# The low parts of split weights computed on VectorE instead of GpSimd in a hybrid decoder step

## The chip, the core and the metric

The kernel runs on one core of one Trainium2 chip. The metric is the time of the program on the device in microseconds; the median of 3 runs of the kernel before is 2004.66 us (1998.97 to 2009.29). The engines are named as in the profile: PE is TensorE (matrix products; PEld its weight loads), DVE is VectorE, ACT is ScalarE, POOL is GpSimd, SP is SyncE, which issues most transfers.

## What is computed

One step of a one-layer decoder for a prompt of 1024 rows and 8 sample rows, with a width of 1024 and float32 inputs. The reference, cut to its frame:

```python
q, k, v, logf, u, z = mixer_inputs(rmsnorm(xp, g_mix), w_in, b_f, g_sgu_v)
xp = xp + merge_heads(fox_prompt(q, k, v, logf), sgu_prompt(u, z, w_s, b_s), g_att_out, g_sgu_out, w_o)
mk, mv = memory_kv(mem_prompt, g_mem, w_ck, w_cv)
xp = xp + cross_attend(rmsnorm(xp, g_cross), mk, mv, w_cq, w_co)
f, conv_p = conv_ffn(rmsnorm(xp, g_ffn), zeros, w_up, conv_w, conv_b, w_down)
xp = xp + f
...
att = fox_sample(q, k, v, logf, cache_k, cache_v, cache_logf, page_table)
...
y_prompt = rmsnorm(xp, g_final); y_sample = rmsnorm(xs, g_final)
```

`fox_prompt` is causal attention with 8 heads of 64 and forget gates, `sgu_prompt` a gating that mixes rows within chunks of 128, `cross_attend` attention with 4 heads into 256 memory rows, and `conv_ffn` a gated MLP (hidden width 2816) with a causal convolution of width 3. The 8 sample rows take the same layer, each attending to 8192 past rows of a paged cache.

## The kernel before

**Split products.** The large products of the prompt run with operands that are split in two: a high part, which ACT writes as a rounded copy (L215), and a low part, the remainder of the source minus the high part (L216). A product is then the sum of three matrix products, high by high, high by low and low by high (`gemm3`, L250, L251, L252; in p1 also L402 to L404). `split` does the splitting. For activations that carry a scale, the remainder is one instruction at L219, always on DVE.

**Weights.** `wload` brings a block of weights of 128 x 1024 (some 128 x 512 or 128 x 1040) into a raw buffer `wr` by a transfer on SP's queue, and calls `split`, which writes `wh` and `wl`. There are 4 raw buffers, 5 for the high and 4 for the low part (`WR`, `WH`, `WL`). `wload` has a kind of weight as argument, and a small table `POOL` says which share of the remainders of a kind is computed on GpSimd: all of `up`, `down` and `o`, none of `p1`. `o` stands for the output projections and the query projection of the cross-attention. An accumulator, `pool_acc`, turns the share into single choices.

**Stages of the prompt.** p1 projects the 1024 rows (to 270 us of the profiled execution or so); then attention and gating for the first half of 512 rows, then attention for the second. From 530 us on, each half goes in turn through the merge of heads and the output projection `out_proj`, the cross-attention `cross`, and the feed-forward `ffn`. In `out_proj` four blocks of weights make up one half of the output columns; four row tiles use all four of them, and a residual addition on DVE (L888) and a sum of squares on ACT (L207) follow each. `rows_rstd` makes the norm's factor from it: an addition (L893), a scaled addition (L200) and a power on GpSimd (L201); `norm_T` scales the rows (L928), transposes on PE (L937, L944) and splits (L218, L219). In the merge the transposes are L834. In `ffn` a block of `w_up` gives one tile of 128 hidden columns: 24 matrix products, then ACT (L1068) and DVE (L1069, L1070) for the convolution, and the product with the gate (L1077), whose result is split (L215, L216). Groups of 6, 6, 5 and 5 pairs of tiles are followed by the products with `w_down` and residual additions (L1102).

**The sample path in the background.** The 128 steps over the cache are interleaved with the prompt at a pace per stage (`PACE`). In each `kstep`, GpSimd issues a gather of 1 MB of keys (L1183), DVE or, for odd steps below 50, GpSimd multiplies by the query (L1191), and DVE sums (L1195). In each `vstep`, GpSimd issues a gather of values (L1244) and PE multiplies by the weights (L1250). Four buffers `kv` serve both. At the end of each of the 8 sample rows a softmax goes back and forth between PE and DVE (L1208, L1214, L1217, L1218, L1220, L1227, L1232, L1238). The rest of the sample path (its projections, cross-attention and feed-forward) follows until the end.

**Order.** Every engine works through its own queue in a fixed order. The order is made ahead of time by a planner that simulates the program: an instruction enters its engine's queue when its inputs and its buffer would be ready, earlier program text first. `tc.issue_after` and `tc.high_priority` change that for some instructions of the sample path and of the residuals.

Of the kernel before, what the change touches and what calls it, by code (L numbers as in the profile page):

```python
# [7 lines left out]
F32 = mybir.dt.float32  # L8
# [10 lines left out]
P = 128  # L19
# [64 lines left out]
def build(nc, tc, ctx, a, phases=None):  # L84
# [121 lines left out]
        j = tpool.tile([P, 1024], BF16, tag="junk", bufs=1, name=nm("junk"))[: src.shape[0], :n]  # L206
        nc.scalar.activation(j, src, AF.Square, accum_out=dst)  # L207

    POOL = {"up": 1.0, "down": 1.0, "p1": 0.0, "o": 1.0}
    pool_acc = [0.0]  # L210

    def split(src, h, l, scale=None, eng=None):

        if scale is None:
            nc.scalar.activation(h, src, AF.Copy)  # L215
            (eng or nc.vector).tensor_tensor(l, src, h.bitcast(F32), op=ALU.subtract)  # L216
        else:
            nc.scalar.activation(h, src, AF.Copy, scale=scale)  # L218
            nc.vector.scalar_tensor_tensor(l, src, scale, h.bitcast(F32), op0=ALU.mult, op1=ALU.subtract)  # L219
# [1 line left out]
    def WRAW(n):  # L221
        return spool.tile([P, SWID], F32, tag="wr", bufs=WR, name=nm("wr"))[:, :n]

    def wload(src, n, kind="p1"):

        pool_acc[0] += POOL[kind]
        eng = nc.vector
        if pool_acc[0] >= 1.0:
            pool_acc[0] -= 1.0
            eng = nc.gpsimd  # L230
        raw = WRAW(n)
        l = spool.tile([P, SWID], F32R, tag="wl", bufs=WL, name=nm("wl"))[:, :n]
        h = spool.tile([P, SWID], F32R, tag="wh", bufs=WH, name=nm("wh"))[:, :n]
        if len(src.shape) == 3:
            h = h.rearrange("p (a b) -> p a b", b=src.shape[2])
            l = l.rearrange("p (a b) -> p a b", b=src.shape[2])
            raw = raw.rearrange("p (a b) -> p a b", b=src.shape[2])
        nc.sync.dma_start(raw, src)
        split(raw, h, l, eng=eng)
        return h, l, raw  # L240

    def wpair(w, kk, c0, n):

        return w[kk * 256 : (kk + 1) * 256, c0 : c0 + n].rearrange("(k p) n -> p k n", p=P)
# [651 lines left out]
    def out_proj(w, mh, ml, xt, fetch=None):  # L896

        sq = squares()
        korder = (4, 5, 6, 7, 0, 1, 2, 3)
        for n in range(2):  # L900
            ws = {}
            for kk in (2, 3, 0, 1):
                ws[kk] = wload(wpair(w, kk, n * 512, 512), 1024, "o")
            if fetch and n == 0:
                xt += fetch()
            for i in range(4):
                tb = slice(i * P, (i + 1) * P)
                ps = MM()
                gemm3(
                    ps[:, :512],  # L910
                    [(mh[k][:, tb], ml[k][:, tb], ws[k // 2][0][:, k % 2, :], ws[k // 2][1][:, k % 2, :]) for k in korder],
                )
                residual(xt, sq, i, n, ps)
                hold[0] = n == 1 and i >= HI
                yield 5.2
        return sq
# [37 lines left out]
    def cross(xt, sq):  # L954

        hs, ls = yield from norm_T(xt, None, G_CROSS)
        r = rows_rstd(sq, 0, 4)
        rq = sm([P, 4], "rq", 2)
        nc.vector.tensor_scalar(rq, r, 1.0 / 16, None, op0=ALU.mult)
        q2 = []  # L960
        for n in range(2):
            ws = [wload(wpair(a["w_cq"], kk, n * 512, 512), 1024, "o") for kk in range(4)]
            for dt_ in range(4):
                if dt_ % 2 == 0:
                    q2.append(U([P, 2, 512]))
                ps = MM()
                cb = slice(dt_ * P, (dt_ + 1) * P)
                gemm3(
                    ps[:, :512],
                    [(ws[k // 2][0][:, k % 2, cb], ws[k // 2][1][:, k % 2, cb], hs[k], ls[k]) for k in range(8)],  # L970
                )
                nc.scalar.activation(q2[-1][:, dt_ % 2, :], ps[:, :512], AF.Copy)
                yield 5.2
        oh, ol = [], []

        def weigh(h):
            mkn = T2().rearrange("p (a b) -> p a b", b=256)
            hc = slice(h * MD, (h + 1) * MD)
            nc.sync.dma_start(mkn, mk_d[:, hc].rearrange("(a p) b -> p a b", p=P))
            mv = T2().rearrange("p (a b) -> p a b", b=256)  # L980
            nc.sync.dma_start(mv, mv_d[:, hc].rearrange("(a p) b -> p a b", p=P))
            tr = TR()
            for dd in range(2):
                for mt in range(2):
                    nc.tensor.transpose(
                        tr[:, dd * 256 + mt * P : dd * 256 + (mt + 1) * P], mkn[:, mt, dd * P : (dd + 1) * P], ident
                    )
            mkT = T2().rearrange("p (a b) -> p a b", b=256)
            nc.scalar.activation(mkT, tr.rearrange("p (a b) -> p a b", b=256), AF.Copy)
            mx = sm([P, 4], "cmx", 2)  # L990
            pp = U([P, 4, 256])
            l4 = sm([P, 4], "cl", 2)
            r4 = sm([P, 4], "cr", 2)
            for g in range(2):
                sv = BK().rearrange("p (i m) -> p i m", m=256)
                for i2 in range(2):
                    i = g * 2 + i2
                    for dd in range(2):
                        mmul(sv[:, i2, :], q2[h][:, dd, i * P : (i + 1) * P], mkT[:, dd, :], start=(dd == 0), stop=(dd == 1))
                g2 = slice(g * 2, g * 2 + 2)  # L1000
                nc.vector.tensor_reduce(mx[:, g2], sv, axis=AX.X, op=ALU.max, negate=True)
                nc.vector.tensor_tensor(mx[:, g2], mx[:, g2], rq[:, g2], op=ALU.mult)
                for i2 in range(2):
                    i = g * 2 + i2
                    nc.scalar.activation(pp[:, i, :], sv[:, i2, :], AF.Exp, bias=mx[:, i : i + 1], scale=rq[:, i : i + 1], accum_out=l4[:, i : i + 1])
            nc.vector.reciprocal(r4, l4)
            for i in range(4):
                nc.vector.tensor_scalar(pp[:, i, :], pp[:, i, :], r4[:, i : i + 1], None, op0=ALU.mult)
            return pp, mv

        def gather(pp, mv):
            pT = U([P, 2, 512])
            for mt in range(2):
                tr = TR()
                for i in range(4):
                    nc.tensor.transpose(tr[:, i * P : (i + 1) * P], pp[:, i, mt * P : (mt + 1) * P], ident)
                nc.scalar.activation(pT[:, mt, :], tr, AF.Copy)
            oh2, ol2 = U([P, 2, 512], F32R), U([P, 2, 512], F32R)
            for dd in range(2):
                ps = BK()  # L1020
                for mt in range(2):
                    mmul(ps, mv[:, mt, dd * P : (dd + 1) * P], pT[:, mt, :], start=(mt == 0), stop=(mt == 1))  # L1022
                split(ps, oh2[:, dd, :], ol2[:, dd, :])
                oh.append(oh2[:, dd, :])
                ol.append(ol2[:, dd, :])

        ahead = weigh(0)
        yield 4
        for h in range(MH):
            cur = ahead  # L1030
            if h < MH - 1:
                ahead = weigh(h + 1)
                yield 4
            gather(*cur)
            yield 5
        return (yield from out_proj(a["w_co"], oh, ol, xt))


    hlast = [const.tile([P, 2 * NF, 2], F32, tag=f"hlast{h}", name=f"hlast{h}") for h in range(2)]

    def ffn(hf, xt, sq, late=None):
# [12 lines left out]
        for gi, gn in enumerate(GROUPS):  # L1054
            gh, gl = [], []
            for f in range(f0, f0 + gn):
                hc2 = []
                for part in range(2):
                    ft = f + part * NF
                    h, l, _ = wload(a["w_up"][ft], 1024, "up")  # L1060
                    hv = h.rearrange("p (k c) -> p k c", c=P)
                    lv = l.rearrange("p (k c) -> p k c", c=P)
                    cw = [gp[:, CW + i * 44 + ft : CW + i * 44 + ft + 1] for i in range(3)]
# [22 lines left out]
            for n in range(2):  # L1086
                ws = []
                for k2 in range(0, gn, 2):
                    m = min(2, gn - k2)
                    r0 = (f0 + k2) * P  # L1090
                    h, l, _ = wload(
                        a["w_down"][r0 : r0 + m * P, n * 512 : (n + 1) * 512].rearrange("(k p) n -> p k n", p=P), m * 512, "down"
                    )
                    for q in range(m):
                        ws.append((h[:, q, :], l[:, q, :]))
                for i in range(4):
                    tb = slice(i * P, (i + 1) * P)
                    ps = MM()
                    gemm3(ps[:, :512], [(gh[k][:, tb], gl[k][:, tb], ws[k][0], ws[k][1]) for k in range(gn)])
                    if f0 + gn < NF:  # L1100
                        xs_ = xt[i][:, n * 512 : (n + 1) * 512]
                        nc.vector.tensor_tensor(xs_, ps[:, :512], xs_, op=ALU.add)  # L1102
                    else:
                        residual(xt, sq, i, n, ps)
                    yield 3.9
# [640 lines left out]
```

## Time and profile before

| | |
|---|---|
| median of 3 runs | 2004.66 us (1998.97 to 2009.29) |
| profiled execution | 1999.7 us, of which the span 1997.9 us |
| mean granted clock of PE | 0.958 |
| busy PE, DVE, POOL, ACT | 92%, 67%, 49%, 37% of the span |
| remainders of weights on POOL (L216) | 184, 450.0 us |
| remainders of weights on DVE (L216) | 36, 51.2 us |
| HBM | 258 GB/s over the span |

The profile is one execution, taken by the hardware profiler. A row of a group has the line of the kernel, the engine, the operation, what it writes and reads (buffer numbers left out), and how often; then the busy time in us and the mean of one in ns, or three durations in ns (minimum, median, maximum). After a second bar stands the idle time of the engine ahead of these instructions and what ended it. A row of the timeline has the start and the duration in us. A row of waits has the total, the number and the longest in us. Busy shares in the row of 40 slices are in tenths, each slice some 50 us. The granted clock is the share of its full rate that PE was given. Spans on POOL are rough.

### The profile page before, as it was taken

What the parts mean: (1) busy time and instruction counts of PE and PEld (TensorE: products, weight loads), DVE (VectorE), ACT (ScalarE), POOL (GpSimd) and SP (SyncE); (2) the same over time, 40 slices, a digit from 0 to 9 for tenths busy, and PEclk for the clock granted to TensorE, in tenths of its full rate; (3) what the DMA queues carried; (4) which work ended last, traced back from release to release, by engine and by line L of the source; (5) the groups of instructions that cost most, each with busy time, mean ns of one, the idle gap of its engine ahead of it and who ended that gap; (6) DMA issues with size and microseconds to landing.
All of it is one profiled execution on the core that took longest, in us unless ns stands there. A gap on an engine that the chain in (4) does not pass through costs nothing.

```text
span 1997.9 us, 24107 instructions
## 1 busy us (share of the span) xinstructions
PE 1838.5 (92%) x9159; PEld 1300.7 (65%) x9159; DVE 1332.5 (67%) x1467; ACT 732.9 (37%) x1344; POOL 988.4 (49%) x560
## 2 busy tenths in 40 slices
PE   8899989778999697999999999789999999899997
PEld 5777766556667455676777667566566668567773
DVE  3877456677677988998879999885424439532232
ACT  5332246566632322332323323322424423232331
POOL 1664343433387547676767576557243344233321
PEclk9999989889999898899999999899999999899999
DMA  8766786754497888888878889878664458666755
GB/s 322 258 235 229 270 318 229 251 172 154 165 356 263 306 296 311 297 309 312 313 279 329 292 296 336 328 259 306 259 225 162 141 192 268 239 197 224 258 204 191
DMA packets 160467, 517.05 MB, mean 259 GB/s; under 512 B 20168, under 2 KB 41928, under 8 KB 127584
## 3 DMA queue, kind: packets, MB, share of 16 engines
q0 software_dynamic: 38528, 270.88, 36.3%
q1 hardware_dynamic: 114912, 232.06, 33.6%
q10 hardware_dynamic: 6912, 12.59, 1.7%
q8 instruction: 72, 1.18, 0.2%
q14 instruction: 43, 0.35, 0.1%
HBM read 493.63 MB, written 21.84 MB: 258 GB/s over the span
## 4 chain that ended last, share of the span: by engine, by line
PE 65%; DVE 18%; DMA 6%; issue 5%; ACT 3%; POOL 2%; SPq 0%; POOLq 0%; ACTq 0%; DVEq 0%
PE ba L250 11%; PE ba L252 11%; PE ba L251 11%; PE bb L250 5%; PE bb L251 5%; PE bb L252 5%; DVE kv L1191 4%; PE dv L1250 4%; DVE s L1195 4%; DMA kv<-cache_k,kidx 2%; POOL wl L216 1%; DVE kv L1414 1%; PE dv L1493 1%; DMA kv<-cache_v,kidx 1%; PE ba L1022 1%
## 5 line engine op out<-in xcount | busy, mean ns | idle before, releaser
L216 POOL TENSOR_TENSOR wl<-wr,wh 128x1024 fp32r<-128x1024 f32 (+1 forms) x184 | 450.0, 2456 | 358.5 <-PE ba L252 211.6
L215 ACT ACTIVATE wh<-wr 128x1024 fp32r<-128x1024 f32 (+2 forms) x220 | 228.1, 1042 | 398.9 <-PE ba L251 105.1
L1191 DVE TENSOR_TENSOR kv<-kv,d 128x2048 f32<-128x2048 f32 (+1 forms) x109 | 308.7, 2836 | 42.6 <-DMA kv<-cache_k,kidx 42.4
L1183 POOL DMA_INDIRECT kv<-cache_k,kidx x128 | 175.8, 1373 | 287.4 <-PE dv L1250 110.3
L1195 DVE TENSOR_REDUCE s<-kv 128x32 f32<-128x2048 f32 (+1 forms) x139 | 292.1, 2107 | 29.4 <-POOL kv L1191 28.2
L1244 POOL DMA_INDIRECT kv<-cache_v,kidx x128 | 184.5, 1441 | 206.7 <-PE dv L1250 96.5
L250 PE MATMUL ba<-wh,u 128*128 128x512 f32 (+1 forms) x674 | 261.9, 390 | 7.1 <-ACT u L215 6.0
L251 PE MATMUL ba<-wl,u 128*128 128x512 f32 (+1 forms) x674 | 258.5, 384 | 1.3 <-DVE wl L216 1.3
L252 PE MATMUL ba<-wh,u 128*128 128x512 f32 (+1 forms) x674 | 257.6, 383 | 0.0
L250 PE MATMUL ba<-u,wh 128*128 128x512 f32 x568 | 231.3, 408 | 0.6 <-DVE u L219 0.5
L252 PE MATMUL ba<-u,wl 128*128 128x512 f32 x568 | 227.2, 401 | 0.0
L251 PE MATMUL ba<-u,wh 128*128 128x512 f32 x568 | 227.2, 400 | 0.0
L250 PEld LDWEIGHTS ba<-wh,u 128*128 128x128 f32 x674 | 128.1, 190 | 52.3 <-issue 17.8
L252 PEld LDWEIGHTS ba<-wh,u 128*128 128x128 f32 x674 | 127.8, 190 | 33.1 <-issue 7.5
L251 PEld LDWEIGHTS ba<-wl,u 128*128 128x128 f32 x674 | 128.2, 190 | 31.7 <-issue 6.5
L1250 PE MATMUL dv<-kv,s 128*32 128x512 f32 x1024 | 137.6, 627 | 5.5 <-DMA kv<-cache_v,kidx 5.5
L250 PEld LDWEIGHTS ba<-u,wh 128*128 128x128 f32 x568 | 108.9, 192 | 49.2 <-issue 14.3
L1191 POOL TENSOR_TENSOR kv<-kv,d 128x2048 f32<-128x2048 f32 (+1 forms) x30 | 117.0, 3908 | 43.9 <-DMA kv<-cache_k,kidx 38.7
L252 PEld LDWEIGHTS ba<-u,wl 128*128 128x128 f32 x568 | 108.5, 191 | 32.8 <-issue 7.6
L251 PEld LDWEIGHTS ba<-u,wh 128*128 128x128 f32 x568 | 108.7, 191 | 31.0 <-issue 5.9
L250 PE MATMUL bb<-wh,u 128*128 128x512 f32 (+1 forms) x318 | 125.5, 395 | 3.1 <-ACT u L215 1.5
L251 PE MATMUL bb<-wl,u 128*128 128x512 f32 (+1 forms) x318 | 123.3, 388 | 2.1 <-DVE wl L216 2.1
(395 smaller groups left out, 3079.1 us busy)
## 6 DMA issues: line engine op xcount, KB each, us to landing
wr<-w_up SPq DMA_DIRECT2D x88, 512.0 KB
kv<-w_up SPq DMA_DIRECT2D x22, 1024.0 KB
wr<-w_down SPq DMA_DIRECT2D x40, 512.0 KB
kv<-w_down SPq DMA_DIRECT2D x11, 1024.0 KB
wr<-w_in SPq DMA_DIRECT2D x16, 512.0 KB
wr<-w_o SPq DMA_DIRECT2D x16, 512.0 KB
wr<-w_cq SPq DMA_DIRECT2D x16, 512.0 KB
wr<-w_co SPq DMA_DIRECT2D x16, 512.0 KB
```

Of the source, the lines that this page charges most:

```text
L215: nc.scalar.activation(h, src, AF.Copy)
L216: (eng or nc.vector).tensor_tensor(l, src, h.bitcast(F32), op=ALU.subtract)
L250: mmul(out, sh, mh, start=(i == 0), stop=False)
L251: mmul(out, sh, ml, start=False, stop=False)
L252: mmul(out, sl, mh, start=False, stop=(i == n - 1))
L1022: mmul(ps, mv[:, mt, dd * P : (dd + 1) * P], pT[:, mt, :], start=(mt == 0), stop=(mt == 1))
L1183: nc.gpsimd.indirect_dma_start(kv, None, a["cache_k"], off(kidx[:, b, ch : ch + 1]))
L1191: eng.tensor_tensor(kvv[:, i : i + m, :], kvv[:, i : i + m, :], qb.unsqueeze(1).broadcast_to((P, m, 512)), op=ALU.mult)
L1195: nc.vector.tensor_reduce(s[:, ch * 4 + i : ch * 4 + i + m, :].rearrange("p k h -> p (k h)"), kvv[:, i : i + m, :].rearrange("p k (h d) -> ...
L1244: nc.gpsimd.indirect_dma_start(kv, None, a["cache_v"], off(kidx[:, b, ch : ch + 1]))
L1250: mmul(dv[32 * j : 32 * j + 32, :], s[:, ch * 4 : ch * 4 + 4, :].rearrange("p k h -> p (k h)"), kvv[:, j, :], start=(ch == 0), stop=(ch == ...
L1414: nc.vector.tensor_tensor(kn, kn, qb[n].unsqueeze(1).broadcast_to((P, 2, 512)), op=ALU.mult)
```

## The change

All remainders of split weights are computed on DVE: the table `POOL`, the accumulator and the arguments that carry them are removed, and `split` has no choice of engine. The 184 remainders at L216 that POOL computed, in `out_proj`, `cross` and `ffn`, go to DVE's queue. GpSimd keeps its gathers, the products of odd early cache steps (L1191), the copies in the attention of half 1 (L686) and the powers (L201). The number of buffers, the transfers and the high parts on ACT stay as they are. The planner makes the order anew.

```diff
-    POOL = {"up": 1.0, "down": 1.0, "p1": 0.0, "o": 1.0}
-    pool_acc = [0.0]
-
-    def split(src, h, l, scale=None, eng=None):
+    def split(src, h, l, scale=None):
 
         if scale is None:
             nc.scalar.activation(h, src, AF.Copy)
-            (eng or nc.vector).tensor_tensor(l, src, h.bitcast(F32), op=ALU.subtract)
+            nc.vector.tensor_tensor(l, src, h.bitcast(F32), op=ALU.subtract)
...
-    def wload(src, n, kind="p1"):
-
-        pool_acc[0] += POOL[kind]
-        eng = nc.vector
-        if pool_acc[0] >= 1.0:
-            pool_acc[0] -= 1.0
-            eng = nc.gpsimd
+    def wload(src, n):
+
...
-        split(raw, h, l, eng=eng)
+        split(raw, h, l)
...
-                ws[kk] = wload(wpair(w, kk, n * 512, 512), 1024, "o")
+                ws[kk] = wload(wpair(w, kk, n * 512, 512), 1024)
...
-            ws = [wload(wpair(a["w_cq"], kk, n * 512, 512), 1024, "o") for kk in range(4)]
+            ws = [wload(wpair(a["w_cq"], kk, n * 512, 512), 1024) for kk in range(4)]
...
-                    h, l, _ = wload(a["w_up"][ft], 1024, "up")
+                    h, l, _ = wload(a["w_up"][ft], 1024)
...
-                        a["w_down"][r0 : r0 + m * P, n * 512 : (n + 1) * 512].rearrange("(k p) n -> p k n", p=P), m * 512, "down"
+                        a["w_down"][r0 : r0 + m * P, n * 512 : (n + 1) * 512].rearrange("(k p) n -> p k n", p=P), m * 512
```

## The prediction

> **What bounds the kernel now.** I read the totals first, then the busy time by stage, the waits of TensorE, and the timeline at its longest waits.
>
> ```profile
> span 1997.9 us, 24107 instructions
> PE 1838.5 (92%) x9159; PEld 1300.7 (65%) x9159; DVE 1332.5 (67%) x1467; ACT 732.9 (37%) x1344; POOL 988.4 (49%) x560
> DVE  3877456677677988998879999885424439532232
> PEclk9999989889999898899999999899999999899999
> ```
> ```profile
> 530.00:590.00 60.00, 59.89 (x327) 44.45 (x325) 41.43 (x44) 26.78 (x50) 44.60 (x22) 1.00 0.94 356
> 590.00:810.00 220.00, 180.95 (x841) 118.20 (x840) 185.27 (x163) 64.63 (x123) 140.81 (x77) 0.89 0.80 295
> 810.00:1250.00 440.00, 432.30 (x1987) 308.27 (x1987) 396.56 (x303) 142.79 (x222) 302.21 (x164) 0.99 0.83 307
> 1250.00:1330.00 80.00, 64.16 (x312) 44.82 (x311) 68.72 (x47) 28.48 (x47) 50.94 (x27) 0.91 0.83 304
> 1330.00:1510.00 180.00, 162.83 (x772) 108.46 (x773) 90.67 (x107) 54.32 (x103) 84.67 (x52) 0.95 0.69 251
> 1510.00:1998.00 488.00, 467.21 (x2348) 327.69 (x2347) 200.40 (x304) 156.95 (x254) 156.79 (x72) 0.98 0.61 210
> ```
> The second block is by stage, with the columns PE, PEld, DVE, ACT, POOL, granted clock, DMA share, GB/s. The stages are: first output projection of half 0; its cross-attention; its feed-forward (810 to 1250); the turn to half 1; its cross-attention; its feed-forward. TensorE bounds the whole, at 92%. Where it isn't full (590 to 810, 1250 to 1510), DVE is what it stands behind, and the clock falls too (0.89, 0.91, 0.95). In the feed-forward of half 0 both run nearly full: PE 432.3 and DVE 396.6 of 440 us.
>
> ```profile
> PE ba L937 <- DVE u L928: 12.9, 2, 6.7
> PE bb L937 <- DVE u L219: 9.2, 2, 4.8
> PE ba L834 <- DVE rn2r L200: 8.9, 1, 8.9
> PE ms L1214 <- DVE pm L1208: 7.7, 2, 6.1
> PE ms L1227 <- DVE dg L1220: 4.4, 3, 3.4
> ```
> These are TensorE's longest waits on DVE from 530 to 1510 us (total, count, longest). None is on the remainder itself. Why DVE was late stands in the timeline; first DVE, then GpSimd, around the 8.9 us wait and around the 6.7 us one:
>
> ```profile
> 1250.24 9.38 DVE L1191 TENSOR_TENSOR kv<-kv,d 128x2048 f32<-128x2048 f32 x1 [1.04 <-DMA kv<-cache_k,kidx]
> 1260.21 2.27 DVE L1195 TENSOR_REDUCE s<-kv 128x32 f32<-128x2048 f32 x1
> 1250.45 7.02 POOL L216 TENSOR_TENSOR wl<-wr,wh 128x1024 fp32r<-128x1024 f32 x3
> 1263.13 1.11 PE L834 MATMUL ba<-cp,u 128*128 128x128 f32 x4 [8.89 <-DVE rn2r L200]
> ...
> 1490.59 11.14 DVE L928 TENSOR_SCALAR u<-u,rn0r 128x1024 f32<-128x1024 f32 x3 [2.48 <-POOL rn0r L201]
> 1490.55 9.30 POOL L216 TENSOR_TENSOR wl<-wr,wh 128x1024 fp32r<-128x1024 f32 x4
> ...
> 593.08 5.26 DVE L893 TENSOR_TENSOR rq<-sqx 128x4 f32<-128x4 f32 x1 [0.85 <-ACT junk L207]
> 588.87 9.45 POOL L216 TENSOR_TENSOR wl<-wr,wh 128x1024 fp32r<-128x1024 f32 x4
> ```
> An addition of four numbers a row (L893) lasts 5.26 us and ends when four GpSimd subtractions end (598.3). A product of 2.28 us (L1191) lasts 9.38 beside three of them. Three scalings (L928), 0.74 each at the median (next block of rows), last 11.14 beside four. GpSimd's remainders hold DVE up, and in bursts, because at the end of a projection three or four buffers come free almost at once. The Trainium skill (SBUF — State Buffer, "Who interferes with whom") has a rule for this: a DVE instruction with two SBUF inputs, or in a two-port mode, and a GpSimd instruction that reads SBUF exclude each other, while a reduction never takes part. The trace agrees: the reduction at 1260.21 takes 2.27 us. By the rule DVE would wait out one GpSimd instruction; 9.38 us is longer than that and covers all three, so the measurement decides.
>
> **What moves, and its price.** Every remainder of a weight from L216 goes from GpSimd's queue to DVE's: 176 of 128x1024 and 8 of 128x512. The p1 stage has 36 on DVE already and doesn't change. No DMA is moved.
>
> ```profile
> L928 DVE TENSOR_SCALAR u<-u,rn0r x6: 734/738/9818, 795.1 to 1501.0; 128x1024 f32<-128x1024 f32 x6
> L216 POOL TENSOR_TENSOR wl<-wr,wh x184: 1284/2413/4481, 536.1 to 1949.3; 128x1024 fp32r<-128x1024 f32 x176, 128x512 fp32r<-128x512 f32 x8
> L216 DVE TENSOR_TENSOR wl<-wr,wh x36: 1208/1226/5641, 8.2 to 343.6; 128x1024 fp32r<-128x1024 f32 x32, 128x1040 fp32r<-128x1040 f32 x4
> L1191 DVE TENSOR_TENSOR kv<-kv,d 128x2048 f32<-128x2048 f32 x97 | 294.5, 3037 | 42.5 <-DMA kv<-cache_k,kidx 42.4
> L1077 DVE TENSOR_TENSOR t<-t,t x44: 659/692/3505, 836.9 to 1935.6; 128x512 f32<-128x512 f32 x44
> L1077 DVE TENSOR_TENSOR t<-t,t 128x512 f32<-128x512 f32 x44 | 45.9, 1042 | 0.8
> L216 DVE TENSOR_TENSOR u<-t,u x44: 669/692/3127, 841.9 to 1937.0; 128x512 fp32r<-128x512 f32 x44
> L216 DVE TENSOR_TENSOR u<-t,u 128x512 fp32r<-128x512 f32 x44 | 43.1, 981 | 14.1 <-ACT u L215 14.1
> ```
> The rows give minimum/median/maximum in ns, or total and mean. One remainder costs GpSimd 2.41 us and DVE 1.23. Added to DVE: 176 x 1.23 + 8 x 0.69 (the same subtraction at 512 wide) = 222 us. Given back to DVE: L1191 97 x (3.04 - 2.28) = 74, L1077 44 x (1.04 - 0.69) = 15, the activations' remainders 44 x (0.98 - 0.69) = 13, L928 9, together 111 us; a little of L1191's is due to GpSimd's own products of the early steps and stays. So DVE's busy time goes to about 1332 + 222 - 111 = 1443 us, 72%. The price is in the stages, not there.
>
> Gain one, the five rows of waits: 12.9 + 9.2 + 8.9 + 6.1 + 3.4 = 40.5 us in seven places (of L1214 and L1227 only the longest; in each DVE had just been held by L216). What is late next there: the same three or four remainders, now 3.7 to 4.9 us of DVE in the same queue. If all stand ahead of the norm's instructions, 7 x 3.7 = 26 us come back and 14.5 are saved; if all stand behind, 40.5. The order isn't shown, but buffers come free while the last product still runs, so more of them will stand ahead than behind; I take two thirds ahead, which saves 23 us. Idle TensorE also costs clock: in the three stages with clocks of 0.89, 0.91 and 0.95 the lost time is 0.11 x 181 + 0.09 x 64 + 0.05 x 163 = 34 us for 39 + 16 + 17 = 72 idle, 0.47 us a us. With it 23 becomes **34 us saved** (21 to 60).
>
> Cost one, the feed-forward of half 0, where DVE has little room:
>
> ```profile
> 810.00:1250.00 440.00, 24.52 (x22) 163.01 (x65) 0.99 0.83 307
> 810.00:1250.00 440.00, 136.63 (x47) 0.00 (x0) 0.99 0.83 307
> 800.00:900.00 100.00, 96.17 (x432) 65.86 (x433) 95.79 (x78) 36.94 (x59) 69.27 (x38) 0.94 0.84 302
> ```
> The first row is of L216 alone (DVE, POOL), the second of L1191 alone, the third of a slice with all engines. 65 remainders add 65 x 1.23 = 80. L1191 gives back 136.6 - 47 x 2.28 = 29.5, and the two 512-wide groups about half of their 28. DVE then needs 396.6 + 80 - 43.5 = 433 of 440 us, 98%. In the third row it was 95.8% busy with TensorE at 96.2%; held to that, 433 / 0.958 = 452, **12 us more** (0 if it fills up, 36 if today's 43.4 us of idle stay beside the 433).
>
> Gain two: GpSimd also issues the gathers of the cache, and waits with them behind its remainders.
>
> ```profile
> PE ba L250 11%; PE ba L252 11%; PE ba L251 11%; PE bb L250 5%; PE bb L251 5%; PE bb L252 5%; DVE kv L1191 4%; PE dv L1250 4%; DVE s L1195 4%; DMA kv<-cache_k,kidx 2%; POOL wl L216 1%; DVE kv L1414 1%; PE dv L1493 1%; DMA kv<-cache_v,kidx 1%; PE ba L1022 1%
> 1051.97 4.62 POOL wl L216 x2
> 1056.91 9.75 DMA kv<-cache_k,kidx
> 1066.68 2.29 DVE kv L1191
> ```
> The chain of waits has 1% of its length, 20 us, in GpSimd's remainders, as here ahead of a gather that DVE then waits for. That goes; between 0 (the buffers free late anyway) and 20 I take **12 us**, which cancels cost one.
>
> Cost two, the 119 remainders outside that stage: each now waits its turn in DVE's queue, behind a cache step of two times 2.28 us, or, after 1510, behind instructions of the sample path that wait on TensorE. Four buffers hide most of it. The nearest rows are those of p1, who waited for the 36 that are on DVE:
>
> ```profile
>   PE bb L251: 2.1, 1
>   PE ba L251: 1.3, 1
> ```
> 3.4 us for 36, 0.094 each: 119 x 0.094 = 11, with the clock's 0.47 **16 us** (0 if the buffers hide all; 32 if DVE, fuller than in p1, doubles it). The waits that GpSimd's remainders had for TensorE's buffers cost nothing there, and DVE inherits them only where the order is wrong; that is within these bounds.
>
> Sum: -34 + 12 - 12 + 16 = -18. Against the profiled execution (1999.7 us, span 1997.9, 1.8 around it) that is 1982; the three runs have a median of 2004.66, 5 us above the profiled one, so the same step from the median gives 1987. The costs are more easily underrated than the gains, since a full in-order engine loses more than one slice shows; I lean 3 us that way: **1990 us**.
>
> **Rivals.** *DVE becomes the bound* (slower). For it: 98% needed from 810 to 1250, with TensorE at 98% beside it, and instructions queued in a fixed order. Against it: the 95.8% slice. If DVE keeps its 43.4 us of idle there, the stage is 36 longer, the rest costs 16 to 32, and of the gains only the 21 come: +31 to +47, so 2036 to 2052. It decides from some 25 us of kept idle on if gain two doesn't come: then costs pass gains (25 - 7 + 16 - 34 = 0, 7 being what 440 - 433 leaves). The Trainium skill (Perfetto Trace Analysis, "Optimizing Scalar/DVE Operations") would favour this rival: with a saturated DVE, handing work even to GpSimd may make sense; it adds that the two share an SBUF read port, so that it might not help.
>
> *Gains and costs cancel*: 34 + 12 against 12 + 32, about 2003. For it: the terms are of one size, and two of them are chosen between ends.
>
> *All remainders fall into DVE's gaps*: -60 - 12 + 0 + 0, 1933; with half of cost two 1941. Against it: the stages with stalls have DVE at 84% and 86%.
>
> *Transfers become the bound*: 307 GB/s over 440 us against the 356 of the stage from 530; the same bytes would fit in 379 us, so no.
>
> **How the numbers follow.** About 0.5% (10 us) is what can be told from no change. The forecast's case, moderate gain between 1960 and 1994, 0.37; the large gain 0.07; cancelling 0.18; DVE as the bound 0.38. So faster 0.44, same 0.18, slower 0.38. Both signs hold much of the chance: the range reaches from 1955 to 2042; the likeliest case's own is 1960 to 1994.
>
> **What would show it.** Right: the longest L1191 after 700 us falls from 9.38 to under 3 us; L893 stays under 1 us and L928 at 0.74; DVE 1420 to 1460 us busy; the five rows of waits at 23 us or less; clock above 0.91 from 590 to 810; the feed-forward of half 0 within 15 us of 440. Wrong: TensorE waiting for wl from DVE by more than 20 us in total, DVE at 97% with TensorE under 95% in that feed-forward, or the norm still late behind a run of L216 on DVE.

## The result and the profile after

| | before | after |
|---|---|---|
| median, 4 runs each | 2001.82 us (1995.63 to 2009.29) | 1973.22 us (1971.44 to 1979.7) |
| ratio, 95% interval | | 0.9874 (0.9843 to 0.9904) |
| span of the profiled execution | 1997.9 us | 1969.6 us |
| mean granted clock | 0.958 | 0.965 |

The change makes the kernel 1.3% faster, 28.6 us between the medians. The prediction had 14.7 us (1990 from 2004.66). Of the 28.3 us between the two spans, 18.6 are idle time of TensorE (159.4 before, 140.8 after) and 9.7 are its busy time: the same 9159 matrix products, at a granted clock of 0.965 instead of 0.958. First the totals of the kernel after, with the busy time in 40 slices. Lines that follow L216 in the text move up by 3 to 8 in it: the remainders of weights are L213, the cache products L1183 (before L1191), the gathers of keys L1175, the residual additions L880, the splits with a scale L216, the norm's scalings L920 and its transposes L929.

```profile
span 1969.6 us, 23939 instructions
PE 1828.8 (93%) x9159; PEld 1295.1 (66%) x9159; DVE 1395.3 (71%) x1651; ACT 730.1 (37%) x1344; POOL 538.0 (27%) x376
DVE  4877466786767798898989999988335549653442
PEclk9999989989999989899999999999999999999998
```

DVE has the 184 remainders more and only 62.8 us more busy time; GpSimd is at 27%. The same groups as before, in the kernel after, by shape (busy us, mean ns, then idle time ahead):

```profile
L213 DVE TENSOR_TENSOR wl<-wr,wh 128x1024 fp32r<-128x1024 f32 x208 | 258.1, 1252 | 168.3 <-PE ba L244 70.1 <-PE bb L244 35.0 <-PE ba L243 17.2
L1183 DVE TENSOR_TENSOR kv<-kv,d 128x2048 f32<-128x2048 f32 x97 | 234.1, 2414 | 24.8 <-DMA kv<-cache_k,kidx 23.7 <-issue 0.9
L1069 DVE TENSOR_TENSOR t<-t,t 128x512 f32<-128x512 f32 x44 | 30.0, 683 | 0.5
L213 DVE TENSOR_TENSOR u<-t,u 128x512 fp32r<-128x512 f32 x44 | 30.0, 684 | 10.9 <-ACT u L212 10.9
L920 DVE TENSOR_SCALAR u<-u,rn0r 128x1024 f32<-128x1024 f32 x6 | 4.1, 748 | 0.8 <-POOL rn0r L201 0.8
```

The groups of the feed-forward and of the norm that had been held are at their own durations again; the cache products are at 2.41 us on average. And here is the view of those products from 700 us on, instruction by instruction (minimum, median, maximum in ns), where GpSimd has no large product left:

```profile
L1183 DVE TENSOR_TENSOR kv<-kv,d x74: 2254/2282/2295, 701.8 to 1371.7; 128x2048 f32<-128x2048 f32 x74
```

None of these is held any more; before, one of 9.38 us stood there. The 62.8 us are what is left of 217.3 added (the remainders of weights on DVE went from 51.2 to 268.5 us in the groups by line), so 154.5 us were given back.

**Where the time came from.** Cut at the same instructions in both timelines (first residual addition of a projection, first and last convolution step on DVE of a feed-forward), in us, one execution of each kernel:

| stretch | before | after | difference |
|---|---|---|---|
| start to the residuals of the first output projection | 558.1 | 556.6 | -1.5 |
| from there, with cross-attention, to the first feed-forward | 270.0 | 272.5 | +2.5 |
| feed-forward of half 0, to its last tile | 397.1 | 381.9 | -15.2 |
| turn to half 1, to the residuals of its first projection | 59.2 | 53.7 | -5.5 |
| cross-attention of half 1 | 232.7 | 225.9 | -6.8 |
| feed-forward of half 1, to its last tile | 416.8 | 414.7 | -2.1 |
| the rest | 64.0 | 64.3 | +0.3 |

More than half comes from the feed-forward of half 0. The busy times of that stretch, before and then after (columns as in the prediction: PE, PEld, DVE, ACT, POOL, clock, DMA share, GB/s):

```profile
828.00:1225.00 397.00, 390.62 (x1807) 280.98 (x1806) 357.45 (x264) 130.05 (x198) 278.15 (x149) 0.99 0.84 308
```
```profile
829.00:1211.00 382.00, 381.11 (x1780) 275.03 (x1779) 357.13 (x319) 128.67 (x199) 124.30 (x83) 1.00 0.81 303
```

DVE is as busy as before, 357 us, although 60.7 us more of remainders are in it (84.5 against 23.8, L213 and L216 alone). The holds paid for most of it: the products of the cache alone take 93.5 us instead of 120. A part is work that now falls outside the cut, such as three of the 43 sums of the cache (6.6 us). TensorE is at 99.8% and the full clock. It, too, has 27 products fewer between the cuts (1780 against 1807), some 6 us (an estimate, by the 0.23 us from one such product to the next in the timeline), and the turn behind has them. The two stretches together are 20.7 us shorter.

**What didn't come.** The first cross-attention gained nothing. Of TensorE's waits on DVE from 530 to 1510 us in the kernel after, these are the longest new ones and what became of the five rows of before:

```profile
PE ba L929 <- DVE u L920: 11.0, 1, 11.0
PE bb L1008 <- DVE u L1000: 3.2, 1, 3.2
PE ba L929 <- DVE u L880: 3.2, 1, 3.2
PE ba L243 <- DVE wl L213: 3.0, 1, 3.0
PE ms L1219 <- DVE dg L1212: 2.6, 1, 2.6
PE bb L929 <- DVE u L216: 2.3, 1, 2.3
PE bb L929 <- DVE u L880: 2.2, 1, 2.2
PE ms L1206 <- DVE pm L1200: 0.5, 1, 0.5
```

The five rows shown before held 43.1 us; their successors, with the 8.9 us one gone altogether, hold 16.4. But one wait of 11 us is left, and others are new, two of them on the residual addition (L880). All rows of TensorE on DVE in that window add up to 59.2 us before and 40.0 after. The timeline around 600 and 795 us (DVE, POOL, then PE) shows why:

```profile
594.39 7.86 DVE L213 TENSOR_TENSOR wl<-wr,wh 128x1024 fp32r<-128x1024 f32 x3
602.17 0.68 DVE L880 TENSOR_TENSOR u<-ba,u 128x512 f32<-128x512 f32 x1
594.81 5.22 POOL L1183 TENSOR_TENSOR kv<-kv,d 128x2048 f32<-128x2048 f32 x1 [1.88 <-DMA kv<-cache_k,kidx]
...
786.21 1.20 DVE L213 TENSOR_TENSOR wl<-wr,wh 128x1024 fp32r<-128x1024 f32 x1
789.75 2.27 DVE L1183 TENSOR_TENSOR kv<-kv,d 128x2048 f32<-128x2048 f32 x1
793.22 0.67 DVE L880 TENSOR_TENSOR u<-ba,u 128x512 f32<-128x512 f32 x1
794.42 0.19 DVE L200 TENSOR_SCALAR rn0r<-rq 128x3 f32<-128x3 f32 x1
799.96 2.29 DVE L1183 TENSOR_TENSOR kv<-kv,d 128x2048 f32<-128x2048 f32 x1 [3.16 <-DMA kv<-cache_k,kidx]
802.83 2.07 DVE L920 TENSOR_SCALAR u<-u,rn0r 128x1024 f32<-128x1024 f32 x3
786.55 7.56 POOL L1175 DMA_INDIRECT kv<-cache_k,kidx  x1 [2.55 <-DVE s L1187]
795.38 0.88 POOL L201 TENSOR_TENSOR rn0r<-rn0r,mhalf 128x3 f32<-128x3 f32 x1
803.63 0.48 PE L929 MATMUL ba<-cp,u 128*128 128x128 f32 x1 [11.03 <-DVE u L920]
```

At 594 us three remainders on DVE, 3.7 us by themselves, take 7.86 because a product of the cache is on GpSimd, which the change leaves there; the residual addition that TensorE waits for stands behind them. At 786 us the hold is turned round: DVE works through remainders and a product without a break, and GpSimd's issue of a gather, else 0.94 us, lasts 7.56. It ends 0.9 us after DVE comes to L880, which reads PSUM. The power of the norm (L201) stands behind it in GpSimd's queue, but that is not what TensorE waits for: the power's input comes from L200, which DVE reaches only at 794.42, behind the remainders and the product, and the power is done at 796.26. The scalings (L920) begin 6.6 us later. Ahead of them in DVE's queue stand a sum of the cache, then 3.16 us of idle time until the late gather has landed, then its product. So the order of DVE's queue makes most of the 11 us; the held issue accounts for the 3.16 us at most, by this timeline.

### The profile page after: what moved, and what is told of

Read it like the earlier page. It is cut to its first block, busy times and chain, and to the rows that moved or that the text cites. A ratio compares the mean times of both kernels' runs of the same rounds, so it can differ in the third digit from the quotient of the medians.

```text
span 1969.6 us, 23939 instructions
## 1 busy us (share of the span) xinstructions
PE 1828.8 (93%) x9159; PEld 1295.1 (66%) x9159; DVE 1395.3 (71%) x1651; ACT 730.1 (37%) x1344; POOL 538.0 (27%) x376
## 4 chain that ended last, share of the span: by engine, by line
PE 71%; DVE 10%; DMA 9%; issue 5%; ACT 3%; POOL 1%; SPq 0%; ACTq 0%; DVEq 0%; POOLq 0%
PE ba L242 12%; PE ba L243 12%; PE ba L244 12%; PE bb L242 6%; PE bb L243 5%; PE bb L244 5%; PE dv L1242 5%; DVE s L1187 2%; DMA wr<-w_in 2%; DVE kv L1183 2%; DMA kv<-cache_k,kidx 2%; DVE wl L213 1%; PE dv L1485 1%; DMA u<-zg_d 1%; PE ba L1014 1%
## 5 line engine op out<-in xcount | busy, mean ns | idle before, releaser
L213 DVE TENSOR_TENSOR wl<-wr,wh 128x1024 fp32r<-128x1024 f32 (+2 forms) x220 | 268.5, 1231 | 176.7 <-PE ba L244 70.1
L1175 POOL DMA_INDIRECT kv<-cache_k,kidx x128 | 174.3, 1362 | 449.1 <-PE dv L1242 208.4
L1183 DVE TENSOR_TENSOR kv<-kv,d 128x2048 f32<-128x2048 f32 (+1 forms) x109 | 248.2, 2282 | 24.8 <-DMA kv<-cache_k,kidx 23.7
L243 PE MATMUL ba<-wl,u 128*128 128x512 f32 (+1 forms) x674 | 258.7, 384 | 3.0 <-DVE wl L213 3.0
L242 PE MATMUL ba<-u,wh 128*128 128x512 f32 x568 | 227.4, 401 | 0.0
L244 PE MATMUL ba<-u,wl 128*128 128x512 f32 x568 | 225.9, 398 | 0.0
L243 PE MATMUL ba<-u,wh 128*128 128x512 f32 x568 | 225.1, 397 | 0.0
L243 PEld LDWEIGHTS ba<-wl,u 128*128 128x128 f32 x674 | 128.1, 190 | 33.9 <-issue 7.1
L1183 POOL TENSOR_TENSOR kv<-kv,d 128x2048 f32<-128x2048 f32 (+1 forms) x30 | 119.3, 3985 | 53.5 <-DMA kv<-cache_k,kidx 47.8
L243 PEld LDWEIGHTS ba<-u,wh 128*128 128x128 f32 x568 | 107.2, 189 | 33.3 <-issue 9.2
L243 PE MATMUL bb<-wl,u 128*128 128x512 f32 (+1 forms) x318 | 122.7, 386 | 1.0 <-DVE wl L213 1.0
```

The source lines that it names most:

```text
L213: nc.vector.tensor_tensor(l, src, h.bitcast(F32), op=ALU.subtract)
L242: mmul(out, sh, mh, start=(i == 0), stop=False)
L243: mmul(out, sh, ml, start=False, stop=False)
L244: mmul(out, sl, mh, start=False, stop=(i == n - 1))
L1175: nc.gpsimd.indirect_dma_start(kv, None, a["cache_k"], off(kidx[:, b, ch : ch + 1]))
L1183: eng.tensor_tensor(kvv[:, i : i + m, :], kvv[:, i : i + m, :], qb.unsqueeze(1).broadcast_to((P, m, 512)), op=ALU.mult)
```

## The experiments

Three theories. **A**: GpSimd's reads of SBUF held DVE, and the gain is that they are gone. **B**: gathers and powers no longer queue behind remainders on GpSimd. **C**: the planner's new order does it, whatever it holds.

**GpSimd busy in the same places, reading or only writing.** Both kernels have DVE's instructions of the kernel after, and GpSimd in front of each of the 184 remainders:

```diff
         nc.scalar.activation(h, raw, AF.Copy)
+        nc.gpsimd.tensor_tensor(l, raw, h.bitcast(F32), op=ALU.subtract)
         nc.vector.tensor_tensor(l, raw, h.bitcast(F32), op=ALU.subtract)
```

> GpSimd subtracts into the low part as in the kernel before, and VectorE then subtracts the same again over it: VectorE's work is that of the kernel after, GpSimd's that of the kernel before. Theory A (the gain is that GpSimd's reads no longer hold VectorE): the holds of 110 to 160 us come back on a VectorE that also has its own 220 us, so 2005 to 2060 us, and the products of the cache steps (L1183 in the kernel after) again show durations of 7 us and more. Theory B (the gain is that gathers and powers no longer queue behind remainders on GpSimd): 2000 to 2030 us. Theory C (the gain is nothing but another planned order): within 10 us of 1973.

The cut is against the kernel after, with `split` written out in `wload`. In the second, the added line is twice `nc.gpsimd.memset(l.bitcast(F32), 0.0)`.

> The same, but GpSimd fills the buffer of the low part twice with zeros instead of subtracting: it is busy at the same places and in the way of the same buffers, but reads nothing from SBUF. Theory A: VectorE isn't held, the mean of the cache products stays near 2.4 us, 1970 to 1992 us, at least 15 us below the run in which GpSimd subtracts. Theory B: as slow as that run, 2000 to 2030 us. Theory C: within 10 us of 1973.

Measured: 2105.67 us, 1.0555 (1.0517 to 1.0593) with GpSimd reading; 1988.5 us, 0.9958 (0.9936 to 0.998) with GpSimd writing. The two rows of DVE and the cache products from 700 us on, first of the kernel that reads, then of the one that writes, with the fills themselves:

```profile
L234 DVE TENSOR_TENSOR wl<-wr,wh 128x1024 fp32r<-128x1024 f32 x176 | 325.1, 1853 | 27.2 <-POOL wl L233 26.9
L1188 DVE TENSOR_TENSOR kv<-kv,d 128x2048 f32<-128x2048 f32 x97 | 278.5, 2872 | 15.4 <-DMA kv<-cache_k,kidx 15.4
L1188 DVE TENSOR_TENSOR kv<-kv,d x77: 2254/2279/7252, 698.7 to 1491.3; 128x2048 f32<-128x2048 f32 x77
```
```profile
L235 DVE TENSOR_TENSOR wl<-wr,wh 128x1024 fp32r<-128x1024 f32 x176 | 213.4, 1219 | 63.7 <-POOL wl L234 53.5 <-PE bb L249 4.5 <-ACT wh L232 3.6
L1189 DVE TENSOR_TENSOR kv<-kv,d 128x2048 f32<-128x2048 f32 x97 | 226.9, 2340 | 31.2 <-DMA kv<-cache_k,kidx 27.8 <-issue 3.4
L1189 DVE TENSOR_TENSOR kv<-kv,d x75: 2268/2285/2300, 697.8 to 1386.9; 128x2048 f32<-128x2048 f32 x75
L234 POOL MEMSET wl<- 128x1024 f32 x176 | 167.9, 960 | 6.1
```

With the same 1651 instructions, DVE is busy for 1621.2 us beside reads and for 1401.6 beside writes. A read holds it, a write does not: a remainder takes 1.85 us in the one and 1.22 in the other, and the longest of the late cache products 7.25 us in the one and 2.30 in the other. GpSimd's two fills are shorter than its subtraction (2 x 0.96 against 2.67 us), but that is not where the 117 us come from: DVE waited 33.0 us for the subtractions and 59.2 for the fills. Theory A had the second right; the first came out 46 us above its range. Theory C's forecast, within 10 us of 1973 for both, failed in both. Theory B has a part: GpSimd in the way of the buffers without reading costs 15 us against the kernel after. Against the kernel before, the writing kernel is only 0.4% faster. So it is shown that the reads cost time, but not how the 28.6 us of the change divide between A and B. The plans of the two kernels differ in the order of PE, DVE and ACT.

**Every remainder twice on DVE** (the last line of `split` once more for these 184).

> The kernel after, with each of the 184 remainders computed twice on VectorE: 222 us more of VectorE, GpSimd unchanged. If VectorE has slack (the added time of the change cost nothing), 1970 to 1985 us. If VectorE is near its limit in the feed-forward of half 0, as the prediction's cost one has it, 65 x 1.23 = 80 us more of VectorE in a stage of 382 us where it is 92% busy: some 50 us there and 16 elsewhere, 2025 to 2060 us.

Measured: 2056.71 us, 1.03 (1.0264 to 1.0337). DVE's own time isn't free: 207 us more of it (1602.5 us busy against 1395.3) cost 83. In the feed-forward of half 0, cut as above:

```profile
841.00:1262.00 421.00, 394.27 (x1782) 277.46 (x1780) 419.45 (x373) 129.17 (x194) 189.29 (x82) 0.98 0.75 276
```

There DVE is the bound, 419.45 of 421 us, and the stage is 39 us longer than with the change. This is the rival that the prediction named, at twice the load.

**GpSimd's products to DVE as well.**

```diff
-KA = 50
+KA = 0
```

> The kernel after, with the products of the first odd cache steps on VectorE too (KA = 0 instead of 50): GpSimd has no large product left. Theory A: 30 products leave that could hold VectorE for 4.6 us each; VectorE gets 30 products of up to 2.28 us, at most 60 us; it is 62 to 75% busy there, so 1955 to 1973 us, and the wait of 3.2 us at 603 us of the profiled execution goes. If VectorE's own time decides in p1 and the attention: 1978 to 1995 us.

Measured: 1946.2 us, 0.9754 (0.9721 to 0.9788), better than expected. The first maximum of the attention on DVE (L701) comes 16.6 us earlier than after the change (278.1 against 294.8 us), and the stretch from the first output projection to the first feed-forward gains 14. All products have their own duration now:

```profile
L1183 DVE TENSOR_TENSOR kv<-kv,d 128x2048 f32<-128x2048 f32 x117 | 266.6, 2283 | 34.5 <-DMA kv<-cache_k,kidx 34.3
```

**The change in parts**: the remainders of the projections, of `w_up`, or of `w_down` alone on DVE, by a 0.0 for that kind in the table `POOL` of the kernel before.

> The kernel before with only the remainders of the projections (kind o: 48 of the 184) on VectorE. The seven long waits of the kernel before stand at the ends of projections: if those holds are the gain (theory A at the norms), most of the 28 us come with this part alone, 1975 to 1987 us. If the gain is in the feed-forward of half 0 (as the milestones of both traces suggest: 15 us there), little comes, 1990 to 2003. If only the new order counts (theory C), anywhere from 1970 to 2005.

> The kernel before with only the remainders of w_up (88 of the 184) on VectorE. The first blocks of w_up are loaded while the projection ahead of them ends, so the bursts beside the norms of the feed-forwards go with this part, and so do most holds in the feed-forward of half 0. Theory A: 1978 to 1992 us. If VectorE's time costs more than the holds gave: 2000 to 2015.

> The kernel before with only the remainders of w_down (40 of their 48 are of 1024, 8 of 512) on VectorE; there are bursts of three at the turns of a group, with cache products of 7 and 9.1 us beside them in the profile of before. Theory A: 1988 to 1998 us. No gain: 1998 to 2008.

Measured: projections 1991.97 us, 0.9969 (0.9943 to 0.9995); `w_up` 1965.27, 0.9831 (0.9806 to 0.9857); `w_down` 1989.71, 0.9939 (0.9905 to 0.9974). `w_up` alone brings at least as much as the whole change (the intervals just overlap) and lies 13 us below its expected range; the parts, 2.6% in all, don't add up to the 1.3%. That moving the projections' remainders alone brings most of the gain is refuted.

**How much does a new order do?** The pace of the sample path in the first feed-forward, 7.8 for 7.5, in the kernel after and in the kernel before.

> The kernel after, with the pace of the sample path in the first feed-forward at 7.8 instead of 7.5: the work is the same, its order is planned anew. It measures how much a new order alone moves the time: theory C needs moves of 15 us or more; theories A and B expect within 8 us of the kernel after (1965 to 1981).

> The kernel before with the pace of the sample path in the first feed-forward at 7.8 instead of 7.5: the same work in a newly planned order, with GpSimd's remainders as they were. If order alone is worth 15 us or more (theory C), 1975 to 1985 or above 2015; otherwise within 8 us of the kernel before.

Measured: 1971.4 us, 0.9861 (0.9829 to 0.9892), beside 0.9874 at the old pace; and 2006.83 us, 1.0063 (1.0035 to 1.0092). Theory C's 15 us were not seen, but 0.6% were. The 117 us between the first two experiments and the 27 us of the products are far from that; the difference between `w_up` alone and the whole change (0.4%), and the sizes for the projections and `w_down`, are not. The change's own 1.3% is twice the larger of only two such moves, so a part of it can be order.

**Remainders and products crossed.**

> The kernel before with only the products of the early cache steps moved to VectorE; all remainders from w_up, w_down and the projections stay on GpSimd. Theory A: the products' holds in p1 and the attention go as in the whole change without products (17 us by the start of the attention, 11 more to its end), the remainders' holds stay: 1970 to 1983 us. If GpSimd's queue is the cause, about the same. If VectorE's time decides: 2000 or more.

> Remainders of w_up and the products of the early cache steps on VectorE; the remainders of the projections and of w_down stay on GpSimd. The part with w_up alone was faster (0.983) than the whole change (0.987), and the whole change without GpSimd's products was at 0.975. If parts add up, 0.983 - 0.012 = 0.971, some 1940 us. If what is left on GpSimd holds VectorE, slower than the whole change without products: 1950 to 1970 us.

Measured: products alone 1982.12 us, 0.9936 (0.9911 to 0.996); `w_up` and products 1945.19, 0.9737 (0.9688 to 0.9786). Products alone bring 0.6%, remainders alone 1.3%, both 2.5%: more than the two together, by no more than a new order moved the time. With the products on DVE it no longer shows whether `w_down` and the projections follow.

**The norm ahead of the remainders.** On the version without GpSimd's products:

```diff
-            with tc.high_priority() if HP and i0 == 3 else nullcontext():
+            with tc.high_priority() if HP else nullcontext():
```

> The kernel after without GpSimd's products (KA = 0), and with the factor of the norm's first three row tiles planned at high priority, as that of the fourth already is: VectorE's L885 and L200 and GpSimd's power should stand ahead of the remainders of the next weights. It bears on the longest wait left, 10.9 us of TensorE at 774 us, where a gather's issue on GpSimd lasted 7.6 us beside a run of VectorE's subtractions and the power stood behind it. If VectorE's order is the cause, the wait falls below 5 us and the time to 1930 to 1942 us. If the held gather ahead of the power is the cause, the wait stays above 7 us and the time within 8 us of 1946.

Measured: 1944.06 us, 0.9717 (0.969 to 0.9744). It tells nothing of the cause: the planner put every engine's instructions in the same order as without the edit. It is a second measurement of that version (0.9754 before), and shows by how much two of them differ. A wait of 10.6 us is there again, with the held issue and the power behind it:

```profile
763.62 7.65 POOL L1175 DMA_INDIRECT kv<-cache_k,kidx  x1 [2.30 <-DVE s L1187]
772.55 0.88 POOL L201 TENSOR_TENSOR rn0r<-rn0r,mhalf 128x3 f32<-128x3 f32 x1
```

In this trace, too, the power is done (773.43) well before the scalings begin (779.45), and a sum of the cache, 2.81 us of waiting for the gather and its product stand between them in DVE's queue. So neither alternative of the expectation is settled, and how much of the wait the held issue costs was not put to a test by an edit.

The fastest versions, 1944 to 1946 us, have no large GpSimd product; they are 1.2 to 1.6% below the kernel after (0.9754, 0.9737 and 0.9717 over 0.9874).

## Why the prediction was right, and where its sizes were off

- **The mechanism was right.** Holds by GpSimd's reads made DVE late; they went with the change, and bringing them back (2105.67 us) against a writing GpSimd (1988.5 us) shows that they cost time. The signs of it came: longest cache product after 700 us 2.3 us, L885 (before L893) 0.16 at most, L920 0.75, the five rows at 16.4 us against "23 or less". Not all signs did: the clock from 590 to 810 us is 0.91, at the bound and not above it; the feed-forward of half 0 moved by 15.2 us, not by 15 or less; and one sign of being wrong, the norm late behind a run of remainders on DVE, is seen at 594 and at 786 us.
- **The sum was near by luck in part.** The gain at the norms was put 23 us too large, the pair of cost one and gain two came out 15 us better than its zero, and cost two 18 us better. The first of these errors takes up most of the other two. The prediction itself gave a slower kernel 0.38, no less than its own case (0.37).
- **One reading was wrong**, though not what it was to show: the reduction at 1260.21 us runs after GpSimd's three subtractions have ended (1257.47), so it shows nothing. Seven other reductions of the cache lie wholly beside subtractions, as the one at 872.27 us, and last 2.27 to 2.29 us: they are not held.
- **DVE's busy time** was forecast at 1443 us and is 1395: 154.5 us were given back, not 111. The four groups of rows in the sum gave 98.5 us. The rest came from the many small ones that were held now and then and that the sum left out, such as L893, whose longest fell from 5.27 to 0.16 us.
- **Gain one** (34 us at the norms) was too large. The five rows fell, but with the new waits TensorE's waiting on DVE fell by 19 us, and the stretches in which they stood gained 1.5 - 2.5 + 5.5 + 6.8 = 11 us. The clock's part was sized about right: 9.7 us of busy time for 18.6 of idle time, 0.52 us a us against 0.47. "What is late next" was the step that fell short: remainders ahead of the norm were priced at 1.23 us each, and at 594 us three cost 7.86 because GpSimd's products still held them. At 786 us they stand ahead of the norm as it feared, but together with steps of the cache, one of which waits for a gather whose issue was held; neither was in the price.
- **Cost one and gain two** (12 less 12) were mis-sized most: -15.2 us measured, some 6 of them by products that fell into the turn. The give-back in that stage was put at 43.5 of the 80 us added, and was most of them: from 810 to 1250 us, the prediction's own window (in which the kernel after gets further), DVE is busy for 409.5 us instead of the 433 forecast. That DVE becomes the bound of this stage was seen only at a load that the kernel after doesn't reach (the double remainders). How much of the 15 is from gathers that leave earlier was not separated.
- **Cost two** (16 us) was too large as well. TensorE waited 4.0 us in all for remainders on DVE (3.0 and 1.0 in the rows L243 on wl), against 3.4 before; the feed-forward of half 1, where most of it was to fall, became 2.1 us shorter. So the buffers hid nearly all of it.
- Of the **rivals**, DVE as the bound and cancelling fell. The large gain's premise, remainders in DVE's gaps, held in the feed-forwards only.

## What to carry to other kernels

Before work is put on GpSimd to relieve VectorE, look at VectorE's durations beside it: a tiny operation that lasts as long as GpSimd's subtraction shows an engine that is held and not relieved. Price a move by what the holds give back in the stage that it is in, small instructions too, and not by the busy shares; and ask what still stands ahead of the urgent instructions in the queue. Then look at what stays on GpSimd: here the products of the cache were worth as much again.

## What the runs showed of the hardware beyond that

- A hold doesn't end with one instruction of the other engine. A product of 2.28 us outlasted three subtractions of GpSimd (9.38 us), and three scalings of 0.74 us four (11.14 us). The page SBUF — State Buffer of the Trainium skill ("Who interferes with whom") calls the shared ports an exclusive lock and says, of VectorE's two-port modes, that whoever issues first has them for the whole instruction while the other is blocked. These traces have whole runs.
- It works both ways, and for descriptors too: GpSimd's issue of a gather took 7.56 and 7.65 us instead of 0.94 beside a run of DVE's subtractions and a product. The same section of the Trainium skill has it that such operations, `tensor_tensor`, do not stall descriptor generation, with a reason that it calls inferred; here the long issue stands side by side with them, and it ends as the run ends. No edit tested it.
- Fills by GpSimd, 0.96 us for 128x1024, held no cache product: from 700 us on none is longer than 2.30 us. That agrees with the same section of the Trainium skill, by which a GpSimd instruction that only writes doesn't contend with such a product.
